# New orders on VectorE and ScalarE in a two-layer encoder: sums of weights, slabs, a tanh and a root's bias

## The chip, the core and the metric

The kernel runs on one core of one Trainium2 chip. Its five engines each work through their own list of instructions in order: TensorE (PE in the profile) multiplies matrices into PSUM, VectorE (DVE) and ScalarE (ACT) do element-wise work, GpSimd (POOL) does element-wise work and issues DMAs, SyncE (SP) issues DMAs. An instruction that needs another engine's result waits, and all behind it on the same engine wait too. The metric is the time of one execution on the device, in microseconds (us); lower is better.

## What is computed

The input is x, 512 rows of 1024 numbers, all fp32. Two layers follow each other. In the first, the mixing step is a stick-breaking attention of 16 heads of 64; in the second it is a gated linear recurrence (RG-LRU). After each there is a feed-forward step with 4096 hidden units and squared ReLU.

```
for layer in (0, 1):
    h = rms_norm(x, norm_mix[layer])
    x = x + (attention(h) if layer == 0 else rglru(h))
    h = rms_norm(x, norm_mlp[layer])
    x = x + (relu(h @ w1[layer]) ** 2) @ w2[layer]
return rms_norm(x, norm_final)

attention: z = q k^T / 8;  w = sigmoid(z) * (product of sigmoid(-z) over the keys after this one);  o = w v @ w_o
rglru:     proj = h @ w_in;  gate = gelu(proj[:, :1024]);  xc = conv4(proj[:, 1024:])
           r, i = sigmoid(xc @ w_a), sigmoid(xc @ w_x)      (16 blocks of 64 x 64)
           a = exp(-8 r softplus(-lam));  b = sqrt(1 - a^2) * i * xc
           hs[t] = a[t] hs[t-1] + b[t];   y = (hs * gate) @ w_o
```

## The kernel before

**Products in halves.** Every fp32 operand is cut into a high half (an fp32r cast, made by ScalarE) and a low half (operand minus high half, made by VectorE). A product is then three matmuls: high times high, low weights times high, high weights times low (`three`, L196 to L198). A slab is a 128x1024 piece of weights: SP loads it into `raw` (three buffers), ScalarE casts `wh` (L184), VectorE subtracts for `wl` (L191). `wh` and `wl` have four buffers each, which come free when TensorE has used them.

**Attention (about 10 to 260 us).** Features lie on partitions. Eight pairs of heads are worked on, staggered: TensorE's order is written out by hand from a list of steps with due times. For each pair there are products for q and k (`qk_steps`), scores (`score_steps`, one VectorE scan each, L542), and `value_steps`: eight turns, in each of which TensorE transposes a block of weights into a PSUM bank `ps_t` (L564), ScalarE copies its high half `th`, and VectorE makes its low half `tl` (L580). Two such banks take turns, and two turns later the halves are multiplied by v (L590, L591). From pair 2 on, the q and k slabs are cut in two pieces of 128x512.

**Feed-forward (260 to 585 and 745 to 1075 us).** Both layers use the class `Mlp`. The hidden units come in four quarters of 1024. The first matrix is a plain product with ReLU and square; the second is a two-by-two block product done with seven products P1 to P7 instead of eight, so some operands are sums: VectorE adds activations (L798, `u`) and weights (L854, `b` or `raw`). Each product has two parts, g = 0 and 1, each with its own weight block: sum if any (L854), high half (ScalarE, L834), low half `wl` (VectorE, L835), twelve matmuls (L866). Results are taken from PSUM to `c` by collects (L875). In the last quarter the order is P1, P5, P2 for g = 0, the same for g = 1, then P6, P3, P7 with both parts each, then P4. There the sums of P7 and P4 (first layer) or of P4 alone (second layer) are done by DMAs that add (`far`, L849), issued from GpSimd. P5's and P6's sums, and P7's in the second layer, are on VectorE, and all but P5's first are held behind `self.ready`, the low half of the last activations (`sl`, L815). The matmuls of P5, g = 1, write `ps_acc`; those of P6 write `ps_t`.

**Recurrence (590 to 720 us).** For each of eight chunks of 128 features: `conv` (a product, four taps, high half `bh` L1064, low half `bl` L1065), `gates` (two small products, L1078 to L1080, two sigmoids L1085 and L1086), `recur` for three chunks together (tanh L1096 and exponential L1098, root L1104, scan L1108), `gate` and `gated` (the GELU side). A change of the kind of function on ScalarE brings a table load (ACT_TABLE_LOAD). GpSimd makes the negative of some slabs' high halves (`wl` L187) and adds the slab by DMA.

**The end.** Transposed to rows, the second layer's sum ends in four blocks of 128 rows. For each, ScalarE squares and adds along the row (`square`, L1177, into `ss`), the root is taken with the part of the sum that was ready first as its bias (`finish`: bias on VectorE L1189, root L1190, reciprocal L1191), and two scaled halves are stored. The last block's last 512 columns come in two halves of 256, whose first sum VectorE adds to `ss` (L1225).

**What sets the order.** On TensorE the program's order holds. On the other four engines a list scheduler orders the instructions from their dependencies, their priorities and its own estimate of durations; `tc.issue_after(x)` makes an instruction stand behind x.

Of the kernel before, what the change touches and what calls it, by code (L numbers as in the profile page):

```python
# [18 lines left out]
S = 512  # L19
# [28 lines left out]
def hybrid_encoder(  # L48
# [38 lines left out]
    def f(ap):  # L87
        return ap.bitcast(F32)
# [174 lines left out]
    with ExitStack() as actx:  # L263
# [74 lines left out]

        def qk_steps(i, pair, then, halves=None, tag="acc"):
            if halves is None:  # L340
                with tc.issue_after(norm["copy"].ins):
                    halves = slab(w_qk[i, pair], CUT)
            wh, wl = halves
            ps = bank(tag)
            for k in range(C):
                xg_step(ps, k, wh, wl)
                if k == C - 1:
                    then(pair, ps)
                yield
# [197 lines left out]
                    w[pair, j, qb] = wt  # L547
                    yield

        lows = []  # L550

        def low():
            pair, o = lows.pop()
# [2 lines left out]
        def value_steps(pair):  # L556
            po, ready, left = {}, {}, {}
            o = None

            def turn(j, kb):  # L560
                n = S - kb * P
                tr = bank("t")
                for qb in range(kb, NB):
                    PE.transpose(  # L564
                        tr[:, (qb - kb) * P : (qb - kb + 1) * P],
                        w[pair, j, qb][:, kb * P : (kb + 1) * P], ident,
                    )
                if kb < NB - 1:
                    th = hp.tile([P, S], F32R, tag="th", name="th", bufs=3)
                    tl = hp.tile([P, S], F32R, tag="tl", name="tl", bufs=3)  # L570
                    dh, dl, q0 = th[:, :n], tl[:, :n], kb * P
                    ready[j, kb] = dh, dl, q0
                else:
                    mh, ml = lasts[j]
                    dh, dl, q0 = mh[:, P:], ml[:, P:], (kb - 1) * P
                    ready[j, kb] = mh, ml, q0

                with tc.high_priority():
                    A.copy(dh, tr[:, :n])
                    left[j, kb] = V.tensor_tensor(dl, tr[:, :n], f(dh), ALU.subtract)  # L580

            def times(j, kb):
                nonlocal o
                if o is None:
                    o = home_tile("osum", 1, "osum")
                if kb == 0:
                    po[j] = bank("o")
                mh, ml, q0 = ready[j, kb]
                vt = v[pair // 2, kb][:, pair % 2 * 2 + j, :]
                PE.matmul(po[j][:, q0:], vt, mh, start=kb == 0, stop=False)  # L590
                PE.matmul(po[j][:, q0:], vt, ml, start=False, stop=kb == NB - 1)  # L591
                if kb == NB - 1:
                    tmp = hp.tile([HD, S], F32, tag="otmp", name="otmp", bufs=1)
                    A.copy(tmp, po[j][HD:, :])
                    V.tensor_tensor(o[half[j], :], po[j][:HD, :], tmp, ALU.add)

            order = [(j, kb) for j in range(2) for kb in range(NB)]
            for i, g in enumerate(order):
                turn(*g)
                yield  # L600
                if i == 1:
                    yield
                if i == 2 and lows:

                    with tc.issue_after(left[order[1]].ins):
                        low()
                if i > 1:
                    times(*order[i - 2])
                    yield
            for g in order[-2:]:  # L610
                times(*g)
                yield
            A.copy(bh[:, pair, :], o)
            lows.append((pair, o))
            if pair == PAIRS - 1:
                low()
            yield
# [101 lines left out]
    class Mlp:  # L719
# [109 lines left out]
        def operand(self, raw):  # L829
            pool = wpools[next(slabs) % len(wpools)]  # L830
            wh = pool.tile([P, C, P], F32R, tag="wh", name="wh")
            wl = pool.tile([P, C, P], F32R, tag="wl", name="wl")
            wh, wl = (t.rearrange("p (j k) f -> p j (k f)", j=2) for t in (wh, wl))
            A.copy(wh, raw)  # L834
            V.tensor_tensor(wl, raw, f(wh), ALU.subtract)  # L835
            return wh, wl

        def block(self, q4, name, g, far):

            _, b, to, *_ = self.PRODUCTS[name]  # L840
            if b == "b21":
                t = wpool.tile([P, C, P], F32, tag="raw", name="raw", bufs=3)
                t = t.rearrange("p (j k) f -> p j (k f)", j=2)
                nc.sync.dma_start(out=t, in_=self.weights(q4, g, b))
                self.raws[b, g] = t
            raw = self.raws[b, g]
            if name in far:

                G.dma_start(out=raw, in_=self.weights(q4, g, to), accum_op=ALU.add)  # L849
            elif to:  # L850

                ahead = not far or (name, g) == ("P5", 0)
                with nullcontext() if ahead else tc.issue_after(self.ready.ins):
                    V.tensor_tensor(raw, raw, self.raws[to, g], ALU.add)  # L854
            return self.operand(raw)

# [23 lines left out]
        def down(self, q4, far=(), end=None):  # L880
# [20 lines left out]
            for g in range(2):  # L901
                for name in ("P1", "P5", "P2"):
                    product(name, g)
            for name in ("P6", "P3", "P7"):
                for g in range(2):
                    product(name, g)
# [85 lines left out]
    with ExitStack() as rctx:  # L992
# [96 lines left out]
        def recur(chunks):  # L1089
            nonlocal mark  # L1090

            for c in chunks:
                a0 = rp2.tile([P, S], F32, tag="a0", name="a0")
                d = rp2.tile([P, S], F32, tag="d", name="d")
                with after(sig):
                    ex = A.activation(om[c], aa[c], AF.Tanh, scale=c4[:, c : c + 1])  # L1096
                with after(ex):
                    ex = A.activation(a0, aa[c], AF.Exp, scale=c8[:, c : c + 1])  # L1098
# [53 lines left out]
    with ExitStack() as mctx:  # L1152
# [19 lines left out]
        ss = lp.tile([P, NB, 3], F32, tag="ss", name="ss")  # L1172
        bias = lp.tile([P, NB], F32, tag="bias", name="bias")

        def square(t, h, i, cols=slice(0, S)):
            junk = work.tile([P, S], F32, tag="sq", name="junk")
            A.activation(  # L1177
                junk[:, cols], mlp.y(t, h)[:, cols], AF.Square, accum_out=ss[:, t, i : i + 1]
            )

        def scaled(t, h, cols=slice(0, S)):
            y = mlp.y(t, h)[:, cols]
# [2 lines left out]
        def finish(t, h, i, cut=None):  # L1185

            ts = slice(t * P, (t + 1) * P)
            rt = work.tile([P, 1], F32, tag="rt", name="rt")
            V.tensor_scalar(bias[:, t : t + 1], ss[:, t, 0:1], 1.0 / D, EPS, ALU.mult, ALU.add)  # L1189
            A.activation(rt, ss[:, t, i : i + 1], AF.Sqrt, bias=bias[:, t : t + 1], scale=1.0 / D)  # L1190
            V.reciprocal(rt, rt)  # L1191
            done, y = mlp.y(t, 1 - h), mlp.y(t, h)
# [9 lines left out]
        def end(ws, xs):  # L1202
            for t in range(2):
                square(t, 0, 0)
                scaled(t, 0)
                square(t, 1, 1)
                finish(t, 1, 1)
            for t in range(2, 4):
                square(t, 1, 0)
# [1 line left out]
            for g in range(2):  # L1211
                mlp.times("P4", g, 0, ws[g], xs[0], False)
            mlp.collect("P4", 0, xs[0])
            square(2, 0, 1)
            finish(2, 0, 1)
            mlp.collect("P4", 1, xs[1])
            for i in range(2):
# [2 lines left out]
                for g in range(2):  # L1220
                    mlp.times("P4", g, 1, ws[g], ps, True, cols)
                mlp.collect("P4", 1, ps, cols)
                square(3, 0, 1 + i, cols)
                if i == 0:
                    V.tensor_tensor(ss[:, 3, 0:1], ss[:, 3, 0:1], ss[:, 3, 1:2], ALU.add)  # L1225
                    scaled(3, 0, cols)
            finish(3, 0, 2, HS)

# [66 lines left out]
```

## Time and profile before

| | |
|---|---|
| median of 3 runs | 1084.49 us (1082.81 to 1085.08) |
| the profiled execution | 1083.88 us |
| its span, first to last instruction | 1081.9 us |
| TensorE busy | 1061.7 us, 98% |
| VectorE, ScalarE, GpSimd busy | 823.7, 569.5 and 171.3 us |
| mean share of DMA bandwidth | 116 GB/s |

In the rows of the profile, "L835 DVE ... wl<-b,wh" is line 835 of the kernel, on VectorE, writing `wl` from `b` and `wh`. A time line's row has the start, the duration (both us), the engine, line and operation, the tiles and shapes, how many such instructions in a row, and in square brackets how long the engine had been idle before and what ended that. A row of the waits has who waited for whom, the total, the number of times and the longest. TensorE's matmuls overlap: a 512-wide one is shown 0.39 us long, while the next starts 0.23 us after it.

### The profile page before, as it was taken

The numbers are of one execution on the slowest core, as the hardware profiler recorded it, in microseconds if no ns is written. First come the engines' busy times: TensorE is split into PE (matmuls) and PEld (weight loads), VectorE is DVE, ScalarE is ACT, GpSimd is POOL, SyncE is SP. The second block draws the span as 40 slices with busy tenths as digits, with TensorE's granted clock in tenths as the row PEclk, the third lists the DMA queues.
The fourth block names the chain that finished last, engine by engine and source line by source line (L and its number), as shares of the span: only waits on it lengthen the run. The fifth ranks groups of instructions, "written<-read, shape, count | busy, mean of one in ns | idle before, by whom it ended". The sixth has DMA issues, their size and how long they took to land.

```text
span 1081.9 us, 13604 instructions
## 1 busy us (share of the span) xinstructions
PE 1061.7 (98%) x4992; PEld 880.2 (81%) x4992; DVE 823.7 (76%) x1078; ACT 569.5 (53%) x823; POOL 171.3 (16%) x199
## 2 busy tenths in 40 slices
PE   8999999999999999999999999999999999999987
PEld 7888888888888888888878777887888888888876
DVE  7788787838796597597687769975686597597686
ACT  7667676726455344344345468853454344344344
POOL 2344344420000000000001564122000000000002
PEclk8999999999999999999999999999999999999999
DMA  6754454426305305305332695252305305305103
GB/s 211 200 137 137 100 157 105 140 96 235 105 9 186 117 3 192 117 1 185 100 84 61 166 217 140 78 175 98 98 23 191 98 20 181 111 20 177 57 13 104
DMA packets 44034, 125.71 MB, mean 116 GB/s; under 512 B 7744, under 2 KB 8512, under 8 KB 43968
## 3 DMA queue, kind: packets, MB, share of 16 engines
q1 hardware_dynamic: 41088, 115.94, 34.4%
q0 software_dynamic: 2304, 8.39, 4.5%
q8 instruction: 39, 0.64, 0.3%
q10 hardware_dynamic: 576, 0.52, 0.1%
q14 instruction: 27, 0.22, 0.1%
HBM read 104.91 MB, written 2.10 MB: 99 GB/s over the span
## 4 chain that ended last, share of the span: by engine, by line
PE 84%; DVE 6%; ACT 5%; DMA 3%; issue 1%; SPq 0%; ACTq 0%; DVEq 0%
PE ps_t L866 10%; PE ps_o L866 6%; PE ps_acc L196 6%; PE ps_acc L197 6%; PE ps_acc L198 6%; PE ps_z L866 6%; PE ps_acc L866 5%; PE ps_o L196 4%; PE ps_o L198 4%; PE ps_o L197 4%; PE ps_t L197 3%; PE ps_t L196 3%; PE ps_t L198 3%; PE ps_z L196 3%; PE ps_z L197 3%; PE ps_z L198 3%
## 5 line engine op out<-in xcount | busy, mean ns | idle before, releaser
L184 ACT CAST wh<-raw 128x1024 fp32r<-128x1024 f32 (+2 forms) x136 | 119.8, 901 | 132.7 <-PE ps_o L198 33.4
L834 ACT CAST wh<-b 128x1024 fp32r<-128x1024 f32 x96 | 100.6, 1051 | 134.1 <-PE ps_o L866 25.0
L191 DVE TENSOR_TENSOR wl<-raw,wh 128x1024 fp32r<-128x1024 f32 (+2 forms) x126 | 131.7, 1062 | 24.9 <-ACT wh L184 24.8
L835 DVE TENSOR_TENSOR wl<-b,wh 128x1024 fp32r<-128x1024 f32 x96 | 117.5, 1226 | 27.0 <-ACT wh L834 26.9
L196 PE MATMUL ps_acc<-xgh,wh 128*128 128x512 f32 x304 | 123.7, 407 | 2.1 <-ACT xgh L115 1.4
L197 PE MATMUL ps_acc<-xgh,wl 128*128 128x512 f32 x304 | 120.2, 395 | 0.3 <-DVE wl L166 0.3
L198 PE MATMUL ps_acc<-xgl,wh 128*128 128x512 f32 x304 | 119.9, 395 | 0.0
L849 POOL DMA_DIRECT2D b<-in_w_dn x6 | 5.4, 903 | 639.6 <-DVE wl L835 316.9
L542 DVE TENSOR_TENSOR_SCAN scan<-keep,later 128x128 f32<-128x128 f32 (+1 forms) x64 | 60.6, 948 | 18.7 <-ACT keep L534 10.3
L196 PE MATMUL ps_o<-xgh,wh 128*128 128x512 f32 x176 | 69.5, 395 | 0.2 <-DVE x L695 0.2
L197 PE MATMUL ps_o<-xgh,wl 128*128 128x512 f32 x176 | 68.6, 390 | 0.0
L198 PE MATMUL ps_o<-xgl,wh 128*128 128x512 f32 x176 | 68.6, 390 | 0.0
L198 PEld LDWEIGHTS ps_acc<-xgl,wh 128*128 128x128 f32 x304 | 57.7, 190 | 12.9 <-DVE xgl L116 0.3
L196 PEld LDWEIGHTS ps_acc<-xgh,wh 128*128 128x128 f32 x304 | 57.8, 190 | 12.8 <-ACT xgh L115 1.8
L788 ACT ACTIVATE u<-u 128x512 f32<-128x512 f32 x64 | 39.3, 629 | 52.5 <-DVE u L787 52.5
L196 PE MATMUL ps_t<-xgh,wh 128*128 128x512 f32 x168 | 66.5, 396 | 0.0
L197 PEld LDWEIGHTS ps_acc<-xgh,wl 128*128 128x128 f32 x304 | 58.0, 191 | 10.2 <-DVE wl L166 0.6
L197 PE MATMUL ps_t<-xgh,wl 128*128 128x512 f32 x168 | 65.7, 391 | 0.0
L198 PE MATMUL ps_t<-xgl,wh 128*128 128x512 f32 x168 | 65.5, 390 | 0.0
L546 POOL TENSOR_TENSOR w<-w,scan 128x128 f32<-128x128 f32 (+1 forms) x64 | 53.4, 836 | 52.4 <-DVE scan L542 49.7
L854 DVE TENSOR_TENSOR b<-b,b 128x1024 f32<-128x1024 f32 x46 | 55.7, 1219 | 0.2
L798 DVE TENSOR_TENSOR u<-u 128x256 f32<-128x256 f32 x128 | 49.5, 420 | 2.6 <-ACT u L788 1.9
(327 smaller groups left out, 2750.9 us busy)
## 6 DMA issues: line engine op xcount, KB each, us to landing
raw<-in_w_m SPq DMA_DIRECT2D x64, 512.0 KB, 3.5
b<-in_w_dn SPq DMA_DIRECT2D x48, 512.0 KB, 3.9
raw<-in_w_dn SPq DMA_DIRECT2D x16, 512.0 KB, 3.6
raw<-in_w_in SPq DMA_DIRECT2D x16, 512.0 KB, 4.3
raw<-in_w_qk SPq DMA_DIRECT2D x12, 512.0 KB, 3.5
wl<-raw POOLq DMA_DIRECT2D x10, 512.0 KB, 5.8
x<-in_xT SPq DMA_DIRECT2D x16, 256.0 KB, 4.3
raw<-in_w_ro SPq DMA_DIRECT2D x8, 512.0 KB, 3.4
```

Source lines behind the costliest of these rows:

```text
L184: A.copy(wh[:, k, :], raw[:, k, :])
L191: V.tensor_tensor(wl[:, k, :], raw[:, k, :], f(wh[:, k, :]), ALU.subtract)
L196: PE.matmul(ps, wh, ah, start=start, stop=False)
L197: PE.matmul(ps, wl, ah, start=False, stop=False)
L198: PE.matmul(ps, wh, al, start=False, stop=stop)
L542: V.tensor_tensor_scan(sc[:, S - n : S][:, ::-1], keep[:, :n][:, ::-1], later[:, S - n :][:, ::-1], 1.0, ALU.mult, ALU.max,)
L546: G.tensor_tensor(wt, wt, sc[:, S - n + 1 : S + 1], ALU.mult)
L798: V.tensor_tensor(u[:, out, :], u[:, x, :], u[:, y, :], op)
L834: A.copy(wh, raw)
L835: V.tensor_tensor(wl, raw, f(wh), ALU.subtract)
L854: V.tensor_tensor(raw, raw, self.raws[to, g], ALU.add)
L866: PE.matmul(ps, x[:, block, ts], y[:, jj, cols], start=first and n == 0, stop=last and n == 2, skip_group_check=not new,)
```

## The change

Four edits, none of which changes what is computed.

- In the last quarter of each layer, sums of weights other than P5's are held behind `self.third`, the low half of P2's second part (the last of the first three products), instead of `self.ready`. P5's second sum stays behind `self.ready`; in the other quarters nothing is held, as before.
- The first tanh of each of the chunks 0 to 2 is also held behind `high`, which at that place is the high half of the convolution of chunk 4.
- The root's bias is made by ScalarE behind each square but the last of a block, by an activation with scale 1/D that adds up over the parts. The four VectorE instructions L1189 and the sum L1225 go; five 128x1 activations come.
- The low halves of q and k slabs (from pair 2 on, once four turns have been issued) are held behind the `tl` of the fourth last turn issued.

The matmuls, the collects and all sizes are as they were. The scheduler moves other instructions as well: on VectorE the order changes in the attention (ten slabs), in both last quarters, in the recurrence and at the end; on ScalarE in the recurrence and at the end; on SP ten loads change places with copies of k's and q's halves; on GpSimd two pairs of neighbours change places. On TensorE the order is the same.

```diff
         def qk_steps(i, pair, then, halves=None, tag="acc"):
             if halves is None:
+                behind[0] = lefts[-4].ins if len(lefts) > 3 else None
                 with tc.issue_after(norm["copy"].ins):
                     halves = slab(w_qk[i, pair], CUT)
+                behind[0] = None
...
-        lows = []
+        lows, lefts = [], []
...
                     left[j, kb] = V.tensor_tensor(dl, tr[:, :n], f(dh), ALU.subtract)
+                lefts.append(left[j, kb])
...
             A.copy(wh, raw)
-            V.tensor_tensor(wl, raw, f(wh), ALU.subtract)
+            self.split_last = V.tensor_tensor(wl, raw, f(wh), ALU.subtract)
...
-                ahead = not far or (name, g) == ("P5", 0)
-                with nullcontext() if ahead else tc.issue_after(self.ready.ins):
+                ahead = None
+                if far and (name, g) != ("P5", 0):
+                    ahead = self.ready if name == "P5" else self.third
+                with tc.issue_after(ahead.ins) if ahead else nullcontext():
                     V.tensor_tensor(raw, raw, self.raws[to, g], ALU.add)
...
             for g in range(2):
                 for name in ("P1", "P5", "P2"):
                     product(name, g)
+            self.third = self.split_last
...
-                with after(sig):
+                with after(sig), after(high if c < 3 else None):
                     ex = A.activation(om[c], aa[c], AF.Tanh, scale=c4[:, c : c + 1])
...
-        def square(t, h, i, cols=slice(0, S)):
+        def square(t, h, i, cols=slice(0, S), end=False):
             junk = work.tile([P, S], F32, tag="sq", name="junk")
             A.activation(
                 junk[:, cols], mlp.y(t, h)[:, cols], AF.Square, accum_out=ss[:, t, i : i + 1]
             )
+            if not end:
+                A.activation(
+                    bias[:, t : t + 1], ss[:, t, i : i + 1], AF.Identity,
+                    bias=bias[:, t : t + 1] if i else eps_t, scale=1.0 / D,
+                )
...
-            V.tensor_scalar(bias[:, t : t + 1], ss[:, t, 0:1], 1.0 / D, EPS, ALU.mult, ALU.add)
             A.activation(rt, ss[:, t, i : i + 1], AF.Sqrt, bias=bias[:, t : t + 1], scale=1.0 / D)
...
-                square(t, 1, 1)
+                square(t, 1, 1, end=True)
...
-            square(2, 0, 1)
+            square(2, 0, 1, end=True)
...
-                square(3, 0, 1 + i, cols)
+                square(3, 0, 1 + i, cols, end=i == 1)
                 if i == 0:
-                    V.tensor_tensor(ss[:, 3, 0:1], ss[:, 3, 0:1], ss[:, 3, 1:2], ALU.add)
                     scaled(3, 0, cols)
```

## The prediction

> **What bounds the kernel now.** I read the page first, then the matrix engine's waits, then the time lines of VectorE and ScalarE around each wait. Last came the order of the changed kernel's instructions on each engine against the old one, which holds no times. On TensorE that order is identical, so only its waits can change.
>
> ```profile
> PE 1061.7 (98%) x4992; PEld 880.2 (81%) x4992; DVE 823.7 (76%) x1078; ACT 569.5 (53%) x823; POOL 171.3 (16%) x199
> ```
>
> ```profile
> PE ps_acc L866 <- DVE wl L835: 3.4, 2, 2.9
> PE ps_t L564 <- DVE tl L580: 2.5, 3, 1.5
> PE ps_z L1080 <- DVE bl L1065: 1.5, 2, 1.1
> PE ps_z L1078 <- ACT bh L1064: 1.4, 1, 1.4
> ```
>
> The columns are total us, times, longest. TensorE (PE) is busy 98% of the span, and these four rows hold nearly 9 of its waits. Whatever this change can bring is in them and in the tail after the last matmul. The first row is the end of each feed-forward layer; its 2.9 is this place in the second layer, VectorE first, PE after it:
>
> ```profile
> 1039.47 2.03 DVE L815 TENSOR_TENSOR sl<-u,sh 128x1792 fp32r<-128x1792 f32 x1 [1.81 <-ACT sh L814]
> 1041.41 4.62 DVE L854 TENSOR_TENSOR b<-b,b 128x1024 f32<-128x1024 f32 x4
> 1045.95 0.68 DVE L875 TENSOR_TENSOR c<-c,ps_t 128x512 f32<-128x512 f32 x1
> 1046.55 1.22 DVE L835 TENSOR_TENSOR wl<-b,wh 128x1024 fp32r<-128x1024 f32 x1
> ...
> 1049.42 1.22 DVE L835 TENSOR_TENSOR wl<-b,wh 128x1024 fp32r<-128x1024 f32 x1
> ```
> ```profile
> 1044.56 0.39 PE L866 MATMUL ps_acc<-wh,sh 128*128 128x512 f32 x1
> 1047.82 0.50 PE L866 MATMUL ps_acc<-wl,sh 128*128 128x512 f32 x1 [2.88 <-DVE wl L835]
> ...
> 1053.39 0.39 PE L866 MATMUL ps_t<-wl,bh 128*128 128x512 f32 x1
> ```
>
> Four sums of weights (`b`) stand ahead of the low half that P5 needs (1046.55). P6's low half (1049.42) is ready long before PE takes it at 1053.39.
>
> **The change part by part.** Times are of the profiled execution: span 1081.9 us, 1083.88 in all.
>
> **Sums behind the three products, second layer.** The new VectorE order after `sl` is: one sum (P5), a collect, P5's low half, a collect, P2's low half, then four sums (two for P6, two for P7), three collects, and only then P6's low half. Nothing is removed. First part: the sum ends at 1042.6; the collect needs P1's last matmul of the first half (starts 1042.97, takes 0.39), so it starts at 1043.40; a collect holds VectorE 0.60, so the low half runs 1044.00 to 1045.22 and PE goes on at 1045.27, not 1047.82: 2.55 earlier. What is late next: collect 0.60 and low half 1.13 bring VectorE to 1046.87; four sums at 1.135 (4.62 for four, less the overlapping end) to 1051.41; three collects to 1053.21; P6's low half, 1.22, to 1054.43. PE wants it at 1050.85 (1053.39 less 2.55) and gets it at 1054.48: a new wait of 3.6, and 1.1 later than now. The first matmul after a wait holds PE 0.34 rather than 0.23 (1047.82 to 1048.16), so **+1.2**. Ends: +0.6 if collects and sums run half a microsecond shorter, +1.6 if longer.
>
> **The same, first layer.** Two sums stood ahead of P5's low half (555.16 x2), costing PE 0.51; P7's sums are DMA there. New: P5's collect waits for P1 (556.77 + 0.39), so the low half ends at 559.03 and PE gains only 0.2 (559.30 to 559.07). Then collect and low half to 560.67, two sums to 562.92, three collects to 564.72, P6's low half to 565.94. PE now takes it at 565.00, so about 1.0 later, and 0.1 for the restart: **+1.1** (ends +0.3, +1.4). Everything behind waits for PE's buffers and shifts with it.
>
> **Tanh behind the convolution's copy.** Before, ScalarE runs tanh (644.82), a table load and five more ahead of the copy `bh`, which PE waits for:
>
> ```profile
> 644.82 0.73 ACT L1096 ACTIVATE om<-aa,c 128x512 f32<-128x512 f32 x1
> 645.55 1.28 ACT L1098 ACT_TABLE_LOAD   x1
> ...
> 649.32 0.60 ACT L1064 CAST bh<-bt 128x512 fp32r<-128x512 f32 x1
> ```
>
> The copy's input is ready at 646.63 (last tap on VectorE: 645.89, 0.74). Behind it: copy to 647.3, `bl` to 648.0, both before PE wants them (648.39, 649.05). Waits of 1.43 and 1.07 and two slow restarts go: 2.7 at this place. But ScalarE idles from 644.9 to 646.6 for it, and the chain behind (tanh, exponentials, roots, a slab's cast) starts 2.4 later (647.2), and ScalarE ends the next sigmoids at 659.9, not 658.0. VectorE has to fit two scans (1.21) and products between those and `bl` of the next convolution. That `bl` runs 663.90 to 664.59 today with PE taking it at 664.65. Undisturbed I get it at 662.9, a gain of 1.75. If the products stretch as the one at 659.87 does (1.51, against 0.68 at 645.29, while GpSimd's `wl` L187 of 2.77 us runs), I get 664.8, no gain. I take the middle, **-0.8**; ends -2.7 and +1.0. Later pieces have over 2 us of room (`bl` 709.80 for a matmul near 713.2).
>
> [...]
>
> **Slabs behind turns.** Ten low halves of q and k weights (two 128x512 pieces each, 0.60 to 0.70 a piece) move 2 to 10 us later on VectorE, behind a transpose's `tl`. Cover: they are ready 12 to 15 us before their matmul (119.32, used at 132.50), so PE never waits for them; their weights' buffers come free later, which holds back loads on SP's queue by as much, and those have as much room, except one: its buffer comes free at 153.2, it lands 3.5 later (the page's DMA issues), and ScalarE's cast of it (156.14) waits some 0.6 with sigmoids behind it that PE takes later. On SP these loads now stand behind the eight copies of k's halves instead of ahead of them, which frees the copies. Gain: at 120.62 PE waited 0.4 for a `tl` behind such a piece. Loss: at 151.4 three slabs now follow one another (six pieces, 3.6), so the next `tl` ends at 156.5 rather than 153.33, and PE's next transposes into that bank, at 156.30, wait 0.2. The L564 waits of the second row stem from other slabs and stay. **-0.2**; ends -0.5 and +4.8 (rival below).
>
> **Root's bias on ScalarE.** The last half row's sum is now:
>
> ```profile
> 1074.47 0.75 DVE L1195 SCALAR_TENSOR_TENSOR c<-c,rt,gb 128x512 f32<-128x512 f32 x1
> 1075.14 0.68 DVE L1225 TENSOR_TENSOR ss<-ss 128x1 f32<-128x1 f32 x1
> 1075.75 0.41 DVE L875 TENSOR_TENSOR c<-c,ps_o 128x256 f32<-128x256 f32 x1
> ```
>
> The sum L1225 goes, and PE's last matmul is done by 1075.1, so the collect starts at 1075.14: 0.6 earlier, as do the last square, root, scaling and store. Five new 128x1 activations of about 0.28 (row rt L1190) lie on ScalarE; the last fits between the copy that ends at 1075.42 and the square at 1075.6. Without that gap it would cost its 0.28. On GpSimd P4's second DMA sum now follows one scaling (1.39): issued near 1057, landed near 1063 (5.8 for such a DMA), used at 1070.9. **-0.6** (ends -0.7, -0.3).
>
> Sum: 1.2 + 1.1 - 0.8 - 0.2 - 0.6 = +0.7, so 1083.9 + 0.7 = **1084.6**. The profiled execution lies 0.6 under the median of three, 1084.49, inside their spread (1082.81 to 1085.08).
>
> **The rivals.**
> **Recurrence pays in full.** The conv's copy gives the whole 2.7 and the next `bl` is on time. For: VectorE stands idle some 0.5 us at times there. Against: it is the tightest pair of rows in that stage (0.06). 1084.6 - 1.9 = 1082.7.
> **Attention turns slower.** The six pieces at 151.4 run as slowly as the pair at 211.23 (2.79 for two) does: 8.4 rather than 3.6, and `tl` ends 8 later than today with 2.96 of room; beyond that room it decides, here by 5. For: such pairs occur (211.23; 99.89, 2.17). Against: GpSimd is idle from 149.2 to 151.9. 1084.6 + 4.8 = 1089.4.
> **The new wait cools the clock.** After the start's wait PE's matmuls stand 0.43 apart, not 0.23, from 9.81 to 15.3: 13 times 0.2, 2.6. If a wait of 3.6 does the same, 1084.6 + 2.6 = 1087.2. Against: 2.88 did not (granted clock 1.00 from 1044 to 1076). [...]
>
> **How the numbers follow.** The forecast holds 0.58 (own range 1083.3 to 1086.2), the full recurrence 0.15, the port rule's +1.0 0.08, attention 0.11, the clock 0.08. About 0.2% (2.2 us) is what a measurement of this kernel can tell from no change: faster is under 1082.3, slower over 1086.7. Faster: half of the full recurrence and a little of the forecast, 0.12. Slower: attention, most of the clock, a little of the others, 0.21. Same: 0.67. The range goes from 1082.0, beyond the full recurrence, to 1087.6, beyond the clock.
>
> **What would show it.** The PE row on `wl` L835 keeps its total, some 4 to 5 us, but moves from `ps_acc` to `ps_t`, with a longest of 3.6; the waits on L1078 and L1080 shrink to under 1 together; L564's stay; L1225 is gone and the tail is 0.6 shorter. I am wrong if P6 does not wait, if `bl` of the sixth convolution comes after 665, or if L564 or the score matmuls wait for over a microsecond near 156.

## The result and the profile after

The changed kernel takes 1088.79 us (median of nine runs, 1086.83 to 1091.63) against 1084.17 for the kernel before (1082.81 to 1085.73): a ratio of 1.0042, interval 1.0030 to 1.0054, or 4.6 us slower. The forecast was 1084.6, its range ended at 1087.6. The profiled execution of the changed kernel took 1087.17 us (span 1085.4), 3.3 over that of the kernel before.

TensorE's waits in the changed kernel (total us, times, longest); lines behind the first edit are numbered 3 to 13 higher than before:

```profile
PE ps_t L873 <- DVE wl L839: 4.5, 2, 3.4
PE ps_t L567 <- DVE tl L583: 3.0, 5, 1.5
PE ps_o L1088 <- DVE bl L1073: 2.1, 1, 2.1
```

The first row is the feed-forward layers' end: it has moved from `ps_acc` (P5) to `ps_t` (P6), 3.4 in the second layer and 1.1 in the first. The two waits of the recurrence near 650 are gone from the list; in their place stand one of 0.4 and one of 2.1 on the halves of the next convolution.

The end of the second layer, VectorE, start and duration in us:

```profile
1044.10 1.22 DVE L861 TENSOR_TENSOR b<-b,b 128x1024 f32<-128x1024 f32 x1
1046.08 0.69 DVE L882 TENSOR_TENSOR c<-c,ps_t 128x512 f32<-128x512 f32 x1 [0.77 <-PE ps_t L873]
1046.69 1.22 DVE L839 TENSOR_TENSOR wl<-b,wh 128x1024 fp32r<-128x1024 f32 x1
...
1049.56 4.62 DVE L861 TENSOR_TENSOR b<-b,b 128x1024 f32<-128x1024 f32 x4
1054.10 1.28 DVE L882 TENSOR_TENSOR c<-c,ps_acc 128x512 f32<-128x512 f32 x2
1055.29 0.68 DVE L882 TENSOR_TENSOR c<-c,ps_z 128x512 f32<-128x512 f32 x1
1055.89 1.22 DVE L839 TENSOR_TENSOR wl<-b,wh 128x1024 fp32r<-128x1024 f32 x1
```

and TensorE there:

```profile
1047.96 0.50 PE L873 MATMUL ps_acc<-wl,sh 128*128 128x512 f32 x1 [0.33 <-DVE wl L839]
1057.16 0.50 PE L873 MATMUL ps_t<-wl,bh 128*128 128x512 f32 x1 [3.45 <-DVE wl L839]
```

P5 now waits 0.33 and not 2.88, and P6 waits 3.45: the four sums stand ahead of its low half. VectorE had no gap in this stretch before; now it stands idle for 0.77 ahead of the first collect, with four sums in its hand that it is not allowed to start.

The recurrence, VectorE:

```profile
661.34 1.21 DVE L1116 TENSOR_TENSOR_SCAN om<-aa,bt 128x512 f32<-128x512 f32 x1
662.48 1.46 DVE L1095 TENSOR_TENSOR bt<-om,bt 128x512 f32<-128x512 f32 x1
663.85 1.21 DVE L1116 TENSOR_TENSOR_SCAN om<-aa,bt 128x512 f32<-128x512 f32 x1
664.99 0.66 DVE L1073 TENSOR_TENSOR bl<-bt,bh 128x512 fp32r<-128x512 f32 x1
```

GpSimd, and then TensorE:

```profile
662.35 2.77 POOL L187 TENSOR_SCALAR wl<-wh 128x1024 fp32r<-128x1024 f32 x1 [3.08 <-ACT wh L184]
```

```profile
665.70 0.50 PE L1088 MATMUL ps_o<-bl,gh 128*128 128x512 f32 x1 [2.15 <-DVE bl L1073]
...
666.60 0.63 PE L1088 MATMUL ps_o<-bl,gh 128*128 128x512 f32 x1
667.02 0.63 PE L196 MATMUL ps_t<-xgh,wh 128*128 128x512 f32 x1
667.45 0.63 PE L197 MATMUL ps_t<-xgh,wl 128*128 128x512 f32 x1
```

`bl` needs only `bh`, which ScalarE ends at 662.77; a product and a scan stand between. Behind the wait the matmuls start 0.43 apart, not 0.23, for seven of them (1.4 us, at 0.2 for each), and the granted clock from 666.60 to 669.59 is 0.50. Such a row of matmuls is called a slow stretch from here on. The windows' row for the ten us around it (busy time of PE, PEld, DVE, ACT, POOL; then TensorE's granted clock, DMA share, GB/s) shows the clock:

```profile
662.00:672.00 10.00, 7.45 (x24) 5.30 (x23) 9.16 (x11) 6.29 (x10) 3.67 (x2) 0.83 0.70 169
```

Added up over the stages, by how far TensorE's matmuls start apart beyond their steady spacing, the changed execution lost more than the old one by 0.7 us in the attention, 1.1 in the first layer, 1.2 in the recurrence (-0.2 from waits, +1.4 from the slow stretch) and 1.2 at the end of the second layer, and the tail is 0.4 shorter: 3.8, of which the start and the rest give 0.3 back; the spans differ by 3.5. These are differences of two single executions. The other executions of the changed kernel are, in the median, 1.6 us longer still.

### The profile page after: what moved, and what is told of

Read it like the earlier page. It is cut to its first block, busy times and chain, and to the rows that moved or that the text cites. A ratio compares the mean times of both kernels' runs of the same rounds, so it can differ in the third digit from the quotient of the medians.

```text
span 1085.4 us, 13595 instructions
## 1 busy us (share of the span) xinstructions
PE 1062.9 (98%) x4992; PEld 880.7 (81%) x4992; DVE 824.3 (76%) x1073; ACT 570.4 (53%) x828; POOL 170.0 (16%) x199
## 4 chain that ended last, share of the span: by engine, by line
PE 83%; DVE 6%; ACT 4%; issue 3%; DMA 2%; POOL 2%; SPq 0%; DVEq 0%; ACTq 0%; POOLq 0%
PE ps_t L873 10%; PE ps_o L873 6%; PE ps_acc L196 6%; PE ps_acc L198 6%; PE ps_acc L197 6%; PE ps_z L873 6%; PE ps_acc L873 5%; PE ps_o L196 4%; PE ps_o L198 4%; PE ps_o L197 4%; PE ps_t L196 3%; PE ps_t L197 3%; PE ps_z L196 3%; PE ps_z L197 3%; PE ps_t L198 3%; PE ps_z L198 3%
## 5 line engine op out<-in xcount | busy, mean ns | idle before, releaser
L191 DVE TENSOR_TENSOR wl<-raw,wh 128x1024 fp32r<-128x1024 f32 (+2 forms) x126 | 135.7, 1095 | 24.7 <-ACT wh L184 24.6
L545 DVE TENSOR_TENSOR_SCAN scan<-keep,later 128x128 f32<-128x128 f32 (+1 forms) x64 | 56.9, 890 | 18.9 <-ACT keep L537 14.0
```

Of the source, the lines that this page charges most:

```text
L191: V.tensor_tensor(wl[:, k, :], raw[:, k, :], f(wh[:, k, :]), ALU.subtract)
L545: V.tensor_tensor_scan(sc[:, S - n : S][:, ::-1], keep[:, :n][:, ::-1], later[:, S - n :][:, ::-1], 1.0, ALU.mult, ALU.max,)
```

## The experiments

Unless said otherwise a kernel is the one before with the edit shown. All ratios are to the kernel before, timed on the same chip beside it. Two theories stood at the start: the loss is the sum of its places, with the recurrence as the wrong term (A), or the parts disturb each other or lose time where the profiled execution does not show it (B).

| run | kernel | median us | ratio, 95% interval | clock, us |
|---|---|---|---|---|
| 1 | tanh alone | 1085.99 | 1.0009 (0.9999 to 1.0019) | +1.5 |
| 2 | later sums alone | 1089.26 | 1.0043 (1.0031 to 1.0055) | +1.2 |
| 3 | slabs alone | 1085.63 | 1.0014 (1.0004 to 1.0024) | +0.7 |
| 4 | root's bias alone | 1083.77 | 0.9997 (0.9987 to 1.0007) | -0.1 |
| 5 | sums spread | 1085.42 | 1.0007 (0.9996 to 1.0019) | -1.5 |
| 6 | later sums, P6's wait filled | 1086.00 | 1.0010 (0.9999 to 1.0021) | -0.8 |
| 7 | tanh, halves first once | 1084.48 | 0.9993 (0.9981 to 1.0005) | +0.2 |
| 8 | 5, 7 and the bias | 1084.85 | 1.0006 (0.9994 to 1.0018) | -0.6 |
| 9 | changed kernel, two waits filled | 1086.58 | 1.0012 (0.9997 to 1.0028) | -2.9 |
| 10 | kernel before, three waits filled | 1082.97 | 0.9982 (0.9971 to 0.9994) | -2.3 |
| 11 | tanh, halves first twice | 1084.18 | 0.9989 (0.9975 to 1.0003) | -0.8 |
| 12 | P7's sums on the DMA | 1081.62 | 0.9962 (0.9949 to 0.9974) | -2.2 |
| 13 | changed kernel, P7's sums on the DMA | 1083.08 | 0.9995 (0.9984 to 1.0005) | -0.9 |
| 14 | 12, the bias, recurrence filled | 1079.90 | 0.9965 (0.9953 to 0.9977) | -1.8 |
| 15 | changed kernel, P6's wait filled | 1086.58 | 1.0017 (1.0003 to 1.0032) | -0.8 |
| 16 | changed kernel, old sums | 1085.29 | 1.0008 (0.9998 to 1.0019) | -0.2 |

The medians come from five chips, so only the ratios can be compared between rows. The last column is worked out from the mean granted clock, which is on record for every execution, profiled or not. Where the granted clock is 0.50 (666.60 to 669.59 of the changed kernel, 9.81 to 15.30 of the kernel before), the matmuls start 0.43 apart and not 0.23, so by estimate (1 - mean clock) x span is at most what an execution loses to the clock; the start and the tail are in it, much alike for all kernels. The kernel before loses 5.1 us in this way (mean clock 0.9953, 138 executions), and the column has how much more (+) or less (-) a kernel loses than the kernel before on the same chip. Each number is sure to 0.9 to 1.5. The changed kernel itself has a mean clock of 0.9951 in nine executions: +0.3, sure to 1.1.

### Runs 1 to 4: each part alone

Of each part, given in full above, one or two lines:

```diff
 # run 1
-                with after(sig):
+                with after(sig), after(high if c < 3 else None):
 # run 2
+                    ahead = self.ready if name == "P5" else self.third
 # run 3
+                behind[0] = lefts[-4].ins if len(lefts) > 3 else None
 # run 4
-            V.tensor_scalar(bias[:, t : t + 1], ss[:, t, 0:1], 1.0 / D, EPS, ALU.mult, ALU.add)
+                A.activation(bias[:, t : t + 1], ss[:, t, i : i + 1], AF.Identity, ...)
```

> The old kernel with one part alone: tanh behind the convolution's copy. Theory A (the recurrence is the step that failed): VectorE's order again puts two scans and a product ahead of the sixth convolution's low half bl, so TensorE waits 2.0 to 2.6 us there and its matmuls then run at 0.43 apart for some 3 us; the two old waits (1.43, 1.07) go. Sum +1.0 to +1.3 us, about 1085.3. Rival B (the late bl comes only together with the shifted layers of the whole change): this part gives the forecast -0.8 us, about 1083.4, and TensorE waits under 1 us for bl.

> The old kernel with one part alone: the later sums of weights held behind three products' halves. Theory A (places add up): P6 waits 3.4 us for its low half in the second layer and 1.1 in the first, the old 2.9 and 0.5 shrink to 0.3 each: +2.4 us, about 1086.6. Rival B (the wait of 3.4 also cools the clock in some executions): the median is 1 to 2 us higher still, 1087.5 to 1088.5, and the spread of the runs is wider than the old kernel's 3 us.

> The old kernel with one part alone: low halves of q and k weights behind a turn's subtraction. Theory A (the changed kernel's trace): +0.6 us between 40 and 240 us, a wait of 0.2 near 155.5 and one of 0.6 for ps_z near 205; about 1084.8. Rival B (the forecast): -0.2, about 1084.0. Rival C: the attention part turned slower in the executions that were not profiled: +2 or more, 1086 or above.

> The old kernel with one part alone: the root's bias on ScalarE. Theory A: the last sum of 128x1 on VectorE is gone, the tail is 0.5 to 0.6 us shorter and nothing else moves: about 1083.6. Rival B (the activation lands ahead of the square, or the DMA sum on GpSimd comes late): 0 or +0.3, about 1084.2 to 1084.5.

The sums alone lose 4.7 us by their ratio, as much as the whole change. The tanh alone loses 1.0, not surely; its wait on `bl` is there (2.16), but this execution shows no slow stretch behind it. TensorE then comes too early for a sigmoid:

```profile
695.31 0.50 PE L196 MATMUL ps_o<-bh,wh 128*128 128x512 f32 x1 [0.41 <-ACT aa L1085]
```

With it the recurrence ends 0.6 later than in the kernel before, though no slow stretch is in it. In the changed kernel and in runs 13, 15 and 16, where a slow stretch follows `bl`, this wait does not come, and the stage ends 1.1 to 1.3 later. The profile of run 1 shows a slow stretch somewhere else, one behind the second layer's old wait of 2.88, which the tanh does not touch; the windows' row of run 1:

```profile
1044.00:1060.00 16.00, 13.12 (x51) 10.41 (x50) 14.84 (x19) 5.90 (x9) 3.75 (x3) 0.89 0.42 67
```

Run 2 has two, one behind the recurrence's old waits, which this part does not touch either, and one behind P6's 3.45:

```profile
645.00:662.00 17.00, 14.51 (x51) 10.99 (x50) 15.56 (x22) 13.56 (x19) 7.64 (x8) 0.80 0.60 152
...
1044.00:1060.00 16.00, 12.22 (x46) 9.29 (x46) 15.23 (x17) 6.62 (x8) 3.39 (x2) 0.89 0.12 15
```

So one profiled execution does not tell whether a wait cools the clock, that is, whether a slow stretch at a granted clock of 0.50 stands behind it. Counted over all profiles in which such a wait stands: the 2.88 of P5 was followed by a slow stretch in three of seven (1.4 to 1.6 us), the recurrence's old 1.43 and 1.07 in three of seven (1.2 to 2.6), the new wait on `bl` in four of five (1.2 to 1.6), P6's 3.45 in one of two (1.6), waits of 2.1 to 2.3 later in the recurrence (runs 7, 8 and 11) in one of three (1.6).

Elsewhere in the 18 profiles such stretches stand only at the start, and in run 8 behind a wait of 1.44 near 25 us.

The slabs alone lose 1.5 us (0.4 to 2.6). Their profile shows a wait of 0.24 near 156 and one of 0.3 at `ps_z`, and held against the one profile of the kernel before, the attention is only 0.2 longer. But that profile is a poor yardstick: of the twelve with the old attention it is the slowest up to 250 us, and they differ by 2.1. On average the six profiles with the new order of slabs reach that point 0.9 later than these twelve (uncertainty 0.7), and 0.6 of it arises behind 125 us (uncertainty 0.3). The wait near 156 stands in all six and in none of the twelve; waits at `ps_z` near 205 stand in both groups. So the slabs cost about 0.9.

The bias shortens the tail, from the start of TensorE's last matmul to the end, from 7.0 to 6.5 us, here and in runs 9 and 13 to 16; its own gain lies within the noise of the ratio. The four ratios alone add up to 0.63%, where the whole change has 0.42%; the difference is sure to about 0.24, so it is not shown that the parts help or disturb each other.

### Runs 6, 15, 9 and 10: the clock, with the waits kept

If the clock is what the waits cost beyond their length, then matmuls that do nothing should bring it back. A tile of zeros is multiplied and added into the bank that TensorE is about to use; no half comes earlier.

```diff
+                    if self.fill and (name, g, i, jj, n) == ("P6", 0, 0, 0, 0):
+                        for _ in range(13):
+                            PE.matmul(ps, zero, wh[:, jj, cols], start=False, stop=False, ...)
```

> The second run's kernel (the sums alone) with 13 matmuls by a tile of zeros, added into P6's own bank, in the wait of 3.45 us that P6 has in the second layer; the result is the same and the low half comes no earlier. 13 x 0.23 = 3.0 us of work, so a wait of 0.4 is left. Theory A (the wait costs more than its length, since it halves the granted clock behind it in many executions, 1.6 us each): the granted clock stays 1.00 from 1044 to 1064, the median falls by 1 to 2 us against 1089.3, to about 1087.5, and it is 2.4 to 3 over the kernel before. Rival B (the excess over the places is something else): no change, 1089 to 1089.5.

> The changed kernel with 13 matmuls by zeros in P6's wait of 3.45 us in the second layer and nothing else; every other instruction keeps its place, and P6's low half comes no earlier. Theory A (the wait cools the clock in most executions, which costs as much again as the place): ratio to the kernel before 1.001 to 1.002 instead of 1.0042, about 1086.2. Rival B (the slow stretch costs what the profiles show, 1.6 us in half of the executions): 1.0035, about 1088. Rival C (no cooling): 1.0042.

> The changed kernel with matmuls by a tile of zeros in its two new waits: 13 in P6's wait of 3.45 us in the second layer, one and eight around the sixth convolution's low half (waits of 0.41 and 2.15). No half comes earlier. Theory A (the waits cool the clock in most executions, and that is what lifts the median 4.6 us over the kernel before although the places in the profiled execution add up to 2.4 without the slow stretch): about 1087.0, 1.5 to 2.5 under the changed kernel, granted clock 1.00 from 645 to 675 and from 1044 to 1064. Rival B (another cause, not in the waits): 1088.5 or more.

> The kernel before with matmuls by zeros in its three longest late waits: five and three in the recurrence (1.43 and 1.07 us), eleven in the second layer (2.88). No half comes earlier. Theory A (the old waits cool the clock too: two of six profiles behind the recurrence's, 2.6 us each, three of five behind the second layer's, 1.6 each): -1.5 to -1.9 us, about 1082.7, and a spread of the runs that is narrower than the 6 us of the kernel before. Rival B (only waits over 3 us cool it): no change, 1084.4.

In run 15 every other instruction keeps its place, and TensorE resumes at the same point of the layer:

```profile
1056.56 0.50 PE L873 MATMUL ps_t<-wl,bh 128*128 128x512 f32 x1 [0.40 <-DVE wl L840]
```

That is 9.21 us after P5's second matmul (1047.35), as in the changed kernel (9.20). Yet its ratio is 1.0017 and not 1.0042: 2.7 us less, with intervals that meet only at their ends. Run 6 gives the same for the sums alone (1.0010 for 1.0043, 3.6 us less). Run 10 fills the old waits of the kernel before: 2.0 us faster than it, all eleven runs within 2.7 us (1082.31 to 1084.99). None of the seven filled places (run 14's among them) is followed by a slow stretch in its profile; the granted clock there is 1.00 (645 to 662 in runs 10 and 14, 662 to 672 in run 9, 1044 to 1060 in runs 6, 9, 10 and 15). In run 9 the scheduler moved instructions behind the recurrence too, and TensorE waits 1.0 us near 698 for a sigmoid, so its gain (1.0012 for 1.0042) may be less than the clock alone would give.

The granted clock of all executions says the same: run 10 loses 2.3 us less to the clock than the kernel before and is 2.0 faster, run 9 loses 2.8 less than the changed kernel, run 15 1.4 less, and run 6 1.9 less than run 2 (each sure to 1.1 to 1.3). That the waits cool the clock, in the kernel before as well, is shown. Filling P6's wait gains 2.7 and 3.6 in the ratios, more than the 1.4 and 1.9 of the clock; the difference is within the uncertainty of about 2, and no run explains it.

It does not follow that the change as a whole cools the clock more. The waits that went had cooled it too, and by the clock on record the changed kernel loses only 0.3 us more than the kernel before (uncertainty 1.1).

### Runs 5, 12, 13 and 16: what the end of a layer waits for

Run 5 holds each sum only behind the half before it, so that three of the four sums no longer stand ahead of P6's first low half.

```diff
                 for g in range(2):
                     product(name, g)
+                    if name == "P6":
+                        self.third = self.split_last
```

> The old kernel with the sums of weights held each behind the half before it: P5's ahead, P6's first behind P2's low half as in the change, but P6's second and P7's only behind P6's own low halves. Theory A (order of VectorE decides): three sums of 1.135 us leave the way of P6's low half, which comes 3.4 us earlier (1.1 in the first layer), so P6 waits under 0.3 and the old 2.9 and 0.5 are 0.3 each: -2.7 us against the kernel before, about 1082.1. Theory A with the clock: the old wait of 2.9 cooled the clock in two of four profiles at 1.5 us, so another -0.7, about 1081.4. Rival B (the collects, not the sums, hold P6 up, or P6's second half is late in its place): a wait of over 1 us stays at P6, about 1083.5.

P6 waits 0.33, as theory A had it, but the time is not 2.7 lower: 1.0007. TensorE's waits behind it in run 5:

```profile
1053.35 0.50 PE L868 MATMUL ps_t<-wl,bh 128*128 128x512 f32 x1 [0.33 <-DVE wl L835]
1056.71 0.50 PE L868 MATMUL ps_t<-wh,sh 128*128 128x512 f32 x1 [0.57 <-ACT wh L834]
1057.97 0.50 PE L868 MATMUL ps_t<-wl,sh 128*128 128x512 f32 x1 [0.76 <-DVE wl L835]
1061.38 0.50 PE L868 MATMUL ps_acc<-wl,bh 128*128 128x512 f32 x1 [0.39 <-DVE wl L835]
```

The late time is spread, not saved: at the end of this layer run 5 loses 3.9 us, the kernel before 3.2; in the first layer it is 1.1 more than before, and the tail is 0.4 longer. Of these 2.2 the clock gives 1.5 back by the table (from 1044 to 1060, with no wait over 0.8 now, the granted clock is 1.00 in this profile); that leaves the 0.7 of the ratio. A reading of this is that VectorE's work ends last there, and that an order which lets it idle ahead of a collect (0.76 in run 5, 0.77 in the changed kernel) adds to it. If that is so, taking sums away must pay where ordering them does not:

```diff
-        mlp.quarters(between, ("P4",), end)
+        mlp.quarters(between, ("P7", "P4"), end)
```

> The kernel before with P7's two sums of weights in the second layer made by GpSimd's accumulating DMA, as the first layer does. Theory A (VectorE's work between 1041 and 1062 is what PE waits for there, so the order of its sums gains nothing but taking sums away does): one of the sums ahead of P5's low half goes at least, two in all, so the wait of 2.88 falls to between 0.6 and 1.75 and 1.1 to 2.3 us are gained, with less cooling 2 to 3: about 1082. Rival B (the DMA sums come late, or P4's behind them in GpSimd's queue): a new wait at P7 or P4 of 1 us or more, 1084 or above.

> The changed kernel with P7's two sums of weights in the second layer made by GpSimd's accumulating DMA. Theory A (VectorE's work sets the end of the layer, and the later sums cost only what they let VectorE stand idle ahead of the first collect): two of the four sums of 1.135 leave the way of P6's low half, its wait falls from 3.45 to about 1.2, and with less cooling the time is 2.3 to 4 under the changed kernel, 1085 to 1086.5, still 3 or more over the twelfth run (1081.6), since the first layer's 1.1 and the recurrence stay. Rival B (it was the order that cost, not the load): P6 still waits over 3 us, 1088 or more.

Run 12: 0.9962, 4.1 us faster. P5 waits 0.61 and not 2.88, and nothing comes late behind it:

```profile
1041.24 2.35 DVE L854 TENSOR_TENSOR b<-b,b 128x1024 f32<-128x1024 f32 x2
1043.52 0.68 DVE L875 TENSOR_TENSOR c<-c,ps_t 128x512 f32<-128x512 f32 x1
1044.11 1.22 DVE L835 TENSOR_TENSOR wl<-b,wh 128x1024 fp32r<-128x1024 f32 x1
```

That is 2.2 us at the place; 2.2 more is what this kernel loses less to the clock (mean 0.9970 against 0.9949), and the two together fit the 4.1. Run 13 does the same to the changed kernel, with the order of the sums kept: P6 waits 1.18 where 1.2 was expected, and the ratio falls from 1.0042 to 0.9995, 5.1 us, again well over the 2.2 of the place; 1.1 more is the clock's, and the 1.8 that are left are about as large as the uncertainty. My expectation for the time, 1085 to 1086.5, was too high by 2. Run 16 puts the old sums back and keeps the other three parts:

```diff
-                    ahead = self.ready if name == "P5" else self.third
+                    ahead = self.ready
```

> The changed kernel with the sums put back behind the last activations' low half as before, the other three parts kept. Theory A (the sums hold most of the loss: 2.3 us at the places and about 1 more of cooled clock than the old wait has): ratio 1.0005 to 1.0015, about 1085.3. Rival B (the parts disturb each other, and the rest is lost elsewhere): 1.003 or more.

1.0008: the later sums hold 0.34% of the 0.42%, or 3.7 us (uncertainty 1.7), of which 2.3 are places. By the clock on record 0.8 are the clock's (uncertainty 1.6); the remaining 0.6 are less than can be told.

### Runs 7, 11 and 8: can the recurrence keep the 2.7?

Run 7 is run 1 with the scans behind the sixth convolution's low half, and the sigmoids of the fifth gates behind its high half; run 11 does so for the second group of chunks too (`c < 6`).

```diff
-            with after(mark), after(begin):
+            with after(mark), after(begin), after(high if c == 4 else None):
...
-                with after(tap if c < 6 else None):
+                with after(low if c < 3 else tap if c < 6 else None):
                     V.tensor_tensor_scan(om[c], aa[c], xc[c], 0.0, ALU.mult, ALU.add)
...
-            (recur, range(3)), (conv, 5), (gates, 4),
+            (recur, range(3)), (conv, 5), (scans, range(3)), (gates, 4),
```

> The first run's kernel (tanh behind the convolution's copy alone) with the three scans behind the sixth convolution's low half bl and the sigmoids of the fifth gates behind its copy bh. Theory A (bl was late because a product of 1.46 and a scan of 1.21 stood ahead of it in VectorE's order): bl is done near 661, the waits of 0.4 and 2.2 us there go, and with them the slow stretch behind them: 2.5 to 3 us under the first run, about 1083.2, some 1.7 under the kernel before. Rival B (VectorE is full from 655 on, so the lateness passes to the next convolution's halves): new waits of 1 to 2 us between 667 and 690, no more than 1 us gained, about 1085. Rival C (GpSimd's 2.77 us holds VectorE's product up whatever the order): bl late by over 1 us again.

> The seventh run's kernel with the second group's three scans behind the eighth convolution's low half as well. Theory A (there too the scans stood ahead of bl; VectorE has room later): the wait of 2.1 us at 688 goes with its restart, so -2.2 against the seventh run and -2.7 against the kernel before at the places, about 1082.0. Rival B (VectorE's work is what ends last, the lateness passes on again): a new wait of 1 us or more between 690 and 720, about 1083.5 to 1084.5.

In run 7 both waits near 662 are gone, with GpSimd's instruction still beside `bl`:

```profile
659.77 0.68 DVE L1065 TENSOR_TENSOR bl<-bt,bh 128x512 fp32r<-128x512 f32 x1
657.96 3.09 POOL L187 TENSOR_SCALAR wl<-wh 128x1024 fp32r<-128x1024 f32 x1 [0.50 <-ACT wh L184]
```

So it was the order that made it late. What GpSimd may add is the stretch of the product ahead of it, 1.46 in the changed kernel and 0.66 here, where it runs after GpSimd's instruction. But TensorE waits at the eighth convolution:

```profile
688.50 0.50 PE L1080 MATMUL ps_o<-bl,gh 128*128 128x512 f32 x1 [2.09 <-DVE bl L1065]
```

Run 11 removes that one, and TensorE waits for a PSUM bank that a sigmoid has to empty first:

```profile
694.36 0.50 PE L196 MATMUL ps_o<-bh,wh 128*128 128x512 f32 x1 [2.26 <-ACT aa L1085]
```

From 640 to 720 TensorE is busy 77.50 us of 80 in the kernel before, 77.01 in run 1, 77.51 in run 7 and 77.35 in run 11. So in the orders tried, some 2.5 to 3 us are waited whichever half is first. Rival B of run 7 was right that the lateness passes on, though further on than it said, and its gain over run 1 is 1.7 by the ratios and not under 1 (uncertainty 1.7). The intervals of runs 7 and 11 both take in 1. Run 8 joins runs 5 and 7 and the bias:

> The old kernel with the spread sums, the reordered recurrence and the root's bias on ScalarE together (no slabs behind turns). Theory A (places add up): -2.7 - 2.0 - 0.5 = -5.2, about 1079.7; with the clock no longer cooled behind the two waits another 0.7 to 1.3, 1078.4 to 1079.0, and a spread of the runs that is narrower. Rival B (the parts disturb each other as later data shift): 1081 or more.

It ends at 1.0006, where -5.2 us was hoped for, since the gains of 2.7 and 2.0 are not there: its profile loses 1.1 in the first layer and 0.7 in the second, and the recurrence's wait (2.12, with a slow stretch) has moved to the eighth convolution.

### Run 14: a faster kernel

> The kernel before with P7's sums on the DMA (twelfth run), matmuls by zeros in the recurrence's two waits (five and three) and the root's bias on ScalarE; nothing else of the change. Places add up: -4.1 of the twelfth run's verdict, -0.5 for the bias, and 0.5 to 0.9 for a clock that is no longer cooled in the recurrence: 1079 to 1080.2 against 1084.5, ratio 0.995 to 0.996, all runs within 3 us. Rival: P4's sum, now the fourth in GpSimd's queue behind a scaling, comes late at the end, and the bias gains nothing: 1081 or more.

P7's sums on the DMA, eight matmuls by zeros in the recurrence's two waits and the bias, without the rest of the change: 1079.90 us (1078.13 to 1082.02), 0.9965, faster than both kernels. By its ratio it is no faster than run 12. Its median is 1.7 lower, but on its chip the kernel before was lower too, by about 2. So neither the filling in the recurrence nor the bias shows a gain of its own here.

## Why the prediction was wrong

The two costs in the sum came as forecast. Of its three gains, 1.6 us together, only the root's came, at 0.4: the tanh's and the slabs' terms turned into costs. And the clock, which the sum left out, belongs in it.

**Sums, second layer (+1.2) and first layer (+1.1).** Right at the places: the profiles give +1.2 and +1.1, P6 waits 3.45 (forecast 3.6) and 1.06 (1.0), behind the very instructions that were named.

**Tanh behind the convolution's copy (-0.8).** This step failed most. The two waits went and the chain behind came 2.4 later, both as worked out. `bl` ended at 665.65, which is 664.3 on the old kernel's time (the stage begins 1.4 later in the changed one), 0.3 before the old 664.59: the slow end of the bracket, not the middle. So TensorE, by then some 3 us earlier than in the old kernel, waits 0.41 and 2.15 there. In run 1, where no slow stretch follows, it waits once more at 695, where the prediction gave later pieces over 2 us of room, and the stage costs +0.6 instead of -0.8; in the changed kernel's profile it costs 1.2 with the slow stretch. Run 1 puts the part at +1.0 (-0.1 to +2.1). The bound was named (`bl`, a product stretched to 1.46, scans), but the middle between "free" and "full" had nothing behind it, and runs 1, 7 and 11 show that in each order tried the stage gives the time back at a later place. The prediction's own sign, `bl` after 665, came, though 1.4 of it is the first layer's delay.

No run shows the term of the "port rule's +1.0", to which the chances give 0.08 and which is as large as the upper end of this step: the scan at 663.85 took its 1.21 inside GpSimd's 2.77 (from 662.35), the one at 661.31 in the kernel before took 1.21 too (GpSimd's 2.77 from 659.81), and in run 7 `bl` took 0.68 and came on time with such an instruction beside it. That run 1 measured +1.0 for the part as well is luck.

**Slabs (-0.2).** This step failed too. The wait of 0.2 near 156 came, but the part costs about 0.9 by the averages of the profiles, and 1.5 by run 3's ratio (0.4 to 2.6). Which instructions hold it beyond that wait stays open. "Attention turns slower" did not happen: the six pieces took 3.86, not 8.4, and no turn waited over 0.3 near 156. The measured 1088.79 lies next to that rival's 1089.4, which the stated range left out; that is luck as well.

**Root's bias (-0.6).** The row is gone and the tail 0.4 shorter. The forecast had the last collect start at 1075.14; TensorE's last matmul starts at 1074.96, and the changed kernel's collect follows that matmul's start by 0.32.

**The clock (left out).** The prediction set the cooling aside with "2.88 did not (granted clock 1.00 from 1044 to 1076)". That was one execution; in three of seven profiles a slow stretch of 1.4 to 1.6 us stands behind the 2.88, and in one of two behind P6's 3.45 (1.6). So what the rival "The new wait cools the clock" describes does occur, and its chance of 0.08 was too low. Its price of +2.6 is too high for a sum of differences, since the waits that go had cooled the clock as well (2.0 us, run 10): the clock on record gives +0.3 for the whole change (uncertainty 1.1), and +0.8 (uncertainty 1.6) for the sums by run 16. Behind waits of 2.1 to 2.9 us too the slow spacing, 0.43 for 0.23, stood in some executions and not in others.

**The whole.** At the places, without a slow stretch, +1.2 +1.1 +0.6 +0.9 -0.4 is 3.4. With 0.3 for the clock it is 3.7, where 4.6 (3.3 to 5.9) was measured and +0.7 was forecast. Of the 3.0 between forecast and account the tanh holds 1.4, the slabs 1.1, the clock 0.3 and the root 0.2. The 0.9 that are left are less than the measurement can tell.

## What to carry to other kernels

Where a stage's helper engine is busy almost without a gap (here VectorE, 16.00 us of 16 from 1044 to 1060 in the kernel before), ask what takes work off that engine before ordering its work anew. Here none of the orders that were tried in the two stages gained clearly (the change, runs 1, 2, 5, 7 and 11), and each moved the wait to another place; taking two sums away gained 4.1 us.

Behind the long late waits of TensorE (2.1 to 3.5 us, or 1.43 and 1.07 close together) a slow stretch of 1.2 to 2.6 us stood in 12 of 24 cases here. So such a wait is to be priced at its length plus that chance, and a wait that goes gives the chance back. One profile is no evidence on this, and no yardstick for a stage that differs by 2 us between executions of the same kernel. Several profiles, the mean granted clock of all executions, or the wait filled with matmuls by zeros are.

## What was not expected of the hardware

Waits of 2.1 to 3.5 us on TensorE (or two of 1.43 and 1.07 with two matmuls between) were followed in 12 of 24 cases by 6 to 13 matmuls at 0.43 us apart, 1.2 to 2.6 us lost at 0.2 for each; the same wait, P5's 2.88, was followed by them in three of seven executions. Where such waits were filled with matmuls by a tile of zeros, the granted clock stayed at 1.00 (645 to 662, 662 to 672 and 1044 to 1060): none of seven filled places was followed by such a stretch, and the kernel before gains 2.0 us by 19 matmuls that compute nothing.
